# First loads of a two-layer decoder trunk: x and the gate-up columns moved to two other DMA queues

## The chip, the cores and the metric

The kernel runs on one core of a Trainium2 chip. The metric is the device time of one execution in microseconds (us), lower is better; the median of three runs is given. The engines are PE (TensorE), DVE (VectorE), ACT (ScalarE), POOL (GpSimd) and SP (SyncE), which here only issues DMAs.

## The reference

The program computes two decoder layers on one sequence of 512 tokens with 1024 features, in float32. Layer 0 mixes tokens by chunked gated linear attention, layer 1 by a sparse attention with three branches; each mixer is followed by a mixture of 16 experts with two chosen per token. Only the beginning of layer 0 matters here, cut from the reference:

```python
proj = x @ w_in                      # q, k, v, g_low (16 columns), r
q, k, v, g_low, r = jnp.split(proj, cuts, axis=-1)
log_a = jax.nn.log_sigmoid((g_low @ w_gate_up + b_gate).astype(f32)) / GLA_TAU
b = jnp.cumsum(chunks(log_a, DK), axis=3)
q_dec = q * jnp.exp(b)
scores = jnp.einsum('bhnid,bhnjd->bhnij', q_dec, k * jnp.exp(-b))
```

## The kernel before, in words

A float32 product is made of three float16 products: every operand is split into a high half (ACT writes it: L231 for x, L178 for a weight) and a low half (DVE subtracts: L232, L180), and PE adds high·high, high·low and low·high.

Weights come in units of 1 MB, 128 partitions by 2048 floats (`fetch`, L166), into three staging buffers `wst`. `split` makes the halves `whl` in four pieces of 512 columns. A staging buffer is free again when DVE has made the last low half of its unit. The unit of W[0], the first to be used, is itself fetched in four pieces (256 KB each), and ahead of each piece the callback `x_in` fetches a quarter of the transposed x (`xs`, 512 KB, L446).

The function `gla` begins so, in the order of the text: the small constants `small_gla` are fetched (L134); ACT makes the low-rank weights `wl` from them (L437), DVE their low half (L438); POOL clears `wgu` (L440); then come the eight loads of x and W[0]; four loads of the gate-up columns `wgu` (L454, 32 KB each); the unit W[2]; and the splits. PE then takes the quarters of x one after the other: per quarter six low-rank products into `low` (L465) and twelve into the two banks of q (L470). ACT copies `low` to `glow` (L475), PE multiplies it by `wgu` (L498), DVE and ACT make the gates from that (L506 to L522), while PE projects k of heads 0 and 1 from W[2] (L247 to L249), and then q and k of heads 2 and 3 from W[1] and W[3], whose splits DVE runs among the gates.

The order of the text is not the order on an engine. A planner of the framework lays the instructions of each engine out before the run, by their place in the text and by when it thinks that their operands are there; an instruction whose operands are late lets later ones pass. The order so made is fixed in the program.

Each DMA that SP or ACT issues signals one of eight completion counters in turn, and the next one on the same counter waits at its issue for the earlier one to land.

Of the kernel before, what the change touches and what calls it, by code (L numbers as in the profile page):

```python
# [22 lines left out]
S = 512  # L23
# [36 lines left out]
class Trunk:  # L60
# [368 lines left out]
    def gla(self):  # L429
        nc, a = self.nc, self.a  # L430
# [8 lines left out]
        wgu = self.tmp([P, 512], F32, "wgu", 1)  # L439
        nc.gpsimd.memset(wgu, 0.0)  # L440
        xT = [self.ph.tile([P, KT, S], F16, name=f"xT{i}", tag="xT", bufs=2) for i in range(2)]
        xs = []

        def x_in(c):
            xs.append(self.xtile("xs"))
            nc.sync.dma_start(xs[c], a["xT"][:, 2 * c * S:(2 * c + 2) * S])  # L446

        def x_split(c):
            k = slice(2 * c, 2 * c + 2)
            self.hilo(xT[0][:, k, :], xT[1][:, k, :], xs[c].rearrange("p (k t) -> p k t", k=2))  # L450

        unit = self.fetch(W[0], cuts=WCH, each=x_in)
        for i in range(4):
            nc.sync.dma_start(wgu[32 * i:32 * i + 16, :], a["gla_gu"])  # L454
        unit2 = self.fetch(W[2])
        wq = [self.split(unit, each=x_split), None]

# [1224 lines left out]
```

## Time and profile before

| | us |
|---|---|
| median of three runs | 954.7 |
| lowest and highest of them | 953.49, 954.93 |
| the profiled execution's own time | 952.24 |
| its span, first to last instruction | 950.5 |
| PE busy in the span | 877.9 (92%) |
| DVE, ACT, POOL busy | 744.7, 555.7, 310.8 |

A profile is one execution; its span begins with the first instruction and times below count from there. "Idle before" is the time in which an engine sat still ahead of an instruction, and the arrow names what ended it. Issues of DMAs are listed under the issuing engine's queue (SPq, ACTq) and are not counted as busy.

### The profile page before, as it was taken

To read this page: it belongs to the slowest core of one execution; us is meant where nothing else is said; L and a number is where in the kernel's file an instruction comes from. 1 tells how busy PE (TensorE), PEld (TensorE's weight loads), DVE (VectorE), ACT (ScalarE), POOL (GpSimd) and SP (SyncE) were. 2 spreads that over 40 slices of the span, in tenths; PEclk is the share of its full clock that TensorE was granted. 3 is DMA by queue.
4 is the path that set the end of the run, shared out by engine and by line. 5 is a ranking of instruction groups with operands and counts; after the bars stand their busy time and mean duration, and the time that the engine had idled before them with its cause. 6 is when DMAs were issued, how large, how long until landed. Compare 5 with 4: busy or idle time off the path is not lost. (4 is left out here: it accounts for less than half of the span.)

```text
span 950.5 us, 26582 instructions
## 1 busy us (share of the span) xinstructions
PE 877.9 (92%) x11218; PEld 718.4 (76%) x11218; DVE 744.7 (78%) x1666; ACT 555.7 (58%) x1174; POOL 310.8 (33%) x349
## 2 busy tenths in 40 slices
PE   6999999996799999899989998999999669999994
PEld 2468888876698989668978885767888568888871
DVE  5972225889899999798678765689777899999967
ACT  4823324424499999724644437784544449999940
POOL 0210021003435241530254524543430348623153
PEclk9999999998899999999999999979999879999997
DMA  8662322072399998871322001120005549999683
GB/s 294 247 205 84 128 90 89 1 300 86 114 374 408 377 378 314 212 205 46 134 89 90 1 3 45 52 85 1 2 2 225 219 180 384 404 369 378 238 156 111
DMA packets 29278, 169.19 MB, mean 178 GB/s; under 512 B 3521, under 2 KB 4161, under 8 KB 12641
## 3 DMA queue, kind: packets, MB, share of 16 engines
q1 hardware_dynamic: 23168, 144.49, 40.0%
q0 software_dynamic: 3072, 12.72, 6.0%
q10 hardware_dynamic: 2912, 10.23, 2.8%
q8 instruction: 90, 1.47, 0.6%
q14 instruction: 36, 0.29, 0.1%
HBM read 153.91 MB, written 13.50 MB: 176 GB/s over the span
## 5 line engine op out<-in xcount | busy, mean ns | idle before, releaser
L834 POOL TENSOR_SCALAR ohe<-icap,rt_px 128x96 f16<-128x96 f32 x112 | 114.1, 1033 | 132.8 <-PE bank L923 124.4
L180 DVE SCALAR_TENSOR_TENSOR whl<-wsu,whl 128x512 f16<-128x512 f32 x192 | 127.2, 714 | 2.9 <-ACT whl L178 2.8
L180 DVE SCALAR_TENSOR_TENSOR whl<-wst,whl 128x512 f16<-128x512 f32 x116 | 75.5, 702 | 67.4 <-ACT whl L178 67.4
L178 ACT ACTIVATE whl<-wsu 128x512 f16<-128x512 f32 x192 | 106.7, 624 | 3.2 <-PE bank L258 3.2
L845 PE MATMUL bank<-ohe,xs 128*128 128x96 f16 x2048 | 99.1, 212 | 6.6 <-DVE ohe L834 5.5
L178 ACT ACTIVATE whl<-wst 128x512 f16<-128x512 f32 x144 | 80.8, 624 | 33.1 <-PE bank L249 9.8
L845 PEld LDWEIGHTS <-xs 128*128 128x128 f16 x2048 | 94.5, 101 | 7.2 <-DVE ohe L834 4.5
L180 DVE SCALAR_TENSOR_TENSOR wha<-wst,wha 128x512 f16<-128x512 f32 x144 | 94.1, 705 | 3.1 <-ACT wha L178 3.0
L258 PE MATMUL bank<-whl,xt 128*128 128x256 f16 x320 | 87.1, 273 | 1.0 <-DVE xt L232 1.0
L256 PE MATMUL bank<-whl,xt 128*128 128x256 f16 x320 | 87.2, 273 | 0.8 <-ACT xt L231 0.7
L257 PE MATMUL bank<-whl,xt 128*128 128x256 f16 x320 | 87.2, 273 | 0.0
L178 ACT ACTIVATE wha<-wst 128x512 f16<-128x512 f32 x144 | 79.8, 623 | 3.4 <-DMA wst<-moe 3.2
L920 PE MATMUL bank<-xh,whl 128*128 128x96 f16 x576 | 75.2, 207 | 0.0
L918 PE MATMUL bank<-xh,whl 128*128 128x96 f16 x576 | 75.2, 207 | 0.0
L919 PE MATMUL bank<-xh,whl 128*128 128x96 f16 x576 | 75.2, 207 | 0.0
L258 PE MATMUL bank<-whl,oT 128*128 128x256 f16 x256 | 69.7, 273 | 1.6 <-DVE oT L232 1.6
L256 PE MATMUL bank<-whl,oT 128*128 128x256 f16 x256 | 69.8, 273 | 0.5 <-ACT oT L231 0.5
L258 PE MATMUL bank<-whl,xT 128*128 128x256 f16 x256 | 69.8, 273 | 0.0
L257 PE MATMUL bank<-whl,xT 128*128 128x256 f16 x256 | 69.8, 273 | 0.0
L256 PE MATMUL bank<-whl,xT 128*128 128x256 f16 x256 | 69.8, 273 | 0.0
L257 PE MATMUL bank<-whl,oT 128*128 128x256 f16 x256 | 69.8, 273 | 0.0
L919 PE MATMUL bank<-xh,wha 128*128 128x96 f16 x448 | 61.3, 210 | 0.8 <-PEq L986 0.8
(405 smaller groups left out, 2751.9 us busy)
## 6 DMA issues: line engine op xcount, KB each, us to landing
wsu<-moe SPq DMA_DIRECT2D x54, 1024.0 KB, 8.2
wst<-moe SPq DMA_DIRECT2D x42, 1024.0 KB, 7.8
wst<-gla_in SPq DMA_DIRECT2D x11, 1024.0 KB, 4.8
yslots<-y ACTq DMA_DIRECT2D x26, 384.0 KB, 7.0
wst<-nsa_in SPq DMA_DIRECT2D x9, 1024.0 KB, 4.9
wst<-gla_out SPq DMA_DIRECT2D x4, 1024.0 KB, 4.7
wha<-nsa_out SPq DMA_DIRECT2D x4, 1024.0 KB, 4.8
xs<-xT SPq DMA_DIRECT2D x4, 512.0 KB, 6.8
```

What stands on the lines that cost most here:

```text
L178: self.hi_ins = nc.scalar.activation(hl[:, 0, s], st[:, s], AF.Copy, scale=WS)
L180: nc.vector.scalar_tensor_tensor(hl[:, 1, s], st[:, s], WS, hl[:, 0, s], op0=OP.mult, op1=OP.subtract)
L256: nc.tensor.matmul(out, xt[0][:, k], w[0][:, s], start=(k == 0), stop=False)
L257: nc.tensor.matmul(out, xt[0][:, k], w[1][:, s], start=False, stop=False)
L258: nc.tensor.matmul(out, xt[1][:, k], w[0][:, s], start=False, stop=(k == KT - 1))
L834: eng.tensor_scalar(part[e][0][:, t], self.icap, self.px[:, t, e:e + 1], None, op0=OP.is_equal)
L845: nc.tensor.matmul(banks[half][:, j * CAP:(j + 1) * CAP], xs[t][:, i, k * P:(k + 1) * P], oh[:, t], start=(j == 0 and t == self.order[0] a ...
L918: nc.tensor.matmul(o, w[0][:, s], xh[:, 0, k], start=(k == 0), stop=False)
L919: nc.tensor.matmul(o, w[1][:, s], xh[:, 0, k], start=False, stop=False)
L920: nc.tensor.matmul(o, w[0][:, s], xh[:, 1, k], start=False, stop=(k == KT - 1))
```

## The change

The four loads of x are issued by ACT in place of SP, and the four loads of the gate-up columns by POOL in place of SP. The weights stay on SP. Nothing else is edited.

```diff
         def x_in(c):
             xs.append(self.xtile("xs"))
-            nc.sync.dma_start(xs[c], a["xT"][:, 2 * c * S:(2 * c + 2) * S])
+            nc.scalar.dma_start(xs[c], a["xT"][:, 2 * c * S:(2 * c + 2) * S])
...
         unit = self.fetch(W[0], cuts=WCH, each=x_in)
         for i in range(4):
-            nc.sync.dma_start(wgu[32 * i:32 * i + 16, :], a["gla_gu"])
+            nc.gpsimd.dma_start(wgu[32 * i:32 * i + 16, :], a["gla_gu"])
         unit2 = self.fetch(W[2])
```

## Rows read from the trace of the kernel before

**Rows 1.** Waits of PE over the whole span: total us, times, longest.

```profile
PE bank L759 <- DVE rt_o L746: 18.8, 4, 6.3
PE bank L465 <- ACT xT L231: 7.4, 1, 7.4
...
PE bank L249 <- DVE whl L180: 1.2, 1, 1.2
```

**Rows 2.** Timeline of PE, 0 to 24 us: start, length, instruction, count.

```profile
7.38 0.58 PE L465 MATMUL bank<-xT,wl 128*32 128x512 f16 x1 [7.38 <-ACT xT L231]
7.90 0.61 PE L470 MATMUL bank<-xT,whl 128*128 128x512 f16 x1
...
9.58 3.74 PE L470 MATMUL bank<-xT,whl 128*128 128x512 f16 x11
13.25 0.61 PE L465 MATMUL bank<-xT,wl 128*32 128x512 f16 x6
...
20.26 2.76 PE L470 MATMUL bank<-xT,whl 128*128 128x512 f16 x12
22.86 1.45 PE L498 MATMUL bank<-glow,wgu 128*128 128x512 f32 x3
```

**Rows 3.** Timeline of ACT, 0 to 24 us.

```profile
2.68 1.28 ACT L437 ACT_TABLE_LOAD   x1 [2.68 <-DMA small_gla<-small_gla]
3.98 0.31 ACT L437 ACTIVATE wl<-small_gla 128x128 f16<-128x128 f32 x1
6.27 1.06 ACT L231 ACTIVATE xT<-xs 128x1024 f16<-128x1024 f32 x1 [1.98 <-DMA xs<-xT]
7.23 0.61 ACT L178 ACTIVATE whl<-wst 128x512 f16<-128x512 f32 x1
8.31 1.06 ACT L231 ACTIVATE xT<-xs 128x1024 f16<-128x1024 f32 x1 [0.46 <-DMA xs<-xT]
...
17.81 2.19 ACT L178 ACTIVATE whl<-wst 128x512 f16<-128x512 f32 x4 [2.54 <-DMA wst<-gla_in]
```

**Rows 4.** Timeline of the SP queue, 0 to 30 us: the issues of DMAs.

```profile
0.81 0.38 SPq L134 DMA_DIRECT2D small_gla<-small_gla  x1
1.25 0.42 SPq L446 DMA_DIRECT2D xs<-xT  x1
1.72 0.42 SPq L166 DMA_DIRECT2D wst<-gla_in  x1
...
6.32 2.95 SPq L454 DMA_DIRECT2D wgu<-gla_gu  x4
10.71 0.35 SPq L166 DMA_DIRECT2D wst<-gla_in  x1
...
15.01 6.31 SPq L166 DMA_DIRECT2D wst<-gla_in  x3
```

**Rows 5.** DMA issues by line, one stretch each: 1.2 to 1.6, 1.6 to 2.1 us; last, to landing.

```profile
xs<-xT SPq DMA_DIRECT2D x1, 512.0 KB, 5.0
...
wst<-gla_in SPq DMA_DIRECT2D x1, 256.0 KB, 5.2
```

**Rows 6.** The line that issues yslots, whole span: ACT's DMA issues, ns min/median/max.

```profile
L959 ACTq DMA_DIRECT2D yslots<-y x26: 310/310/349, 263.8 to 900.3; - x26
```

**Rows 7.** Timeline of POOL, 0 to 90 us.

```profile
0.95 0.53 POOL L440 MEMSET wgu<- 128x512 f32 x1
...
2.46 0.23 POOL L483 IOTA io<- 128x128 int32 x1
40.49 0.41 POOL L539 COPY q<-qd 128x256 f32<-128x256 f32 x1 [37.80 <-DVE dec L522]
```

**Rows 8.** DMA issues by line, whole span, a row issued by POOL; last, to landing.

```profile
wst<-ck POOLq DMA_DIRECT2D x2, 1024.0 KB, 10.9
```

**Rows 9.** Timeline of DVE, 0 to 24 us.

```profile
1.41 0.48 DVE L480 MEMSET seg<- 128x512 f32 x1
...
4.32 0.29 DVE L438 SCALAR_TENSOR_TENSOR wl<-small_gla,wl 128x128 f16<-128x128 f32 x1 [2.28 <-ACT wl L437]
```

**Rows 10.** Timeline of DVE, 20 to 60 us.

```profile
21.41 0.17 DVE L672 TENSOR_SCALAR br<-br 128x16 f32<-128x16 f32 x1
23.92 0.75 DVE L506 TENSOR_SCALAR gate<-bank,small_gla 128x512 f32<-128x512 f32 x1 [2.35 <-PE bank L498]
...
28.49 0.68 DVE L180 SCALAR_TENSOR_TENSOR whl<-wst,whl 128x512 f16<-128x512 f32 x1
...
29.69 1.89 DVE L180 SCALAR_TENSOR_TENSOR whl<-wst,whl 128x512 f16<-128x512 f32 x3
...
45.41 0.68 DVE L180 SCALAR_TENSOR_TENSOR whl<-wst,whl 128x512 f16<-128x512 f32 x1
```

**Rows 11.** Timeline of ACT, 20 to 60 us.

```profile
22.95 0.63 ACT L178 ACTIVATE whl<-wst 128x512 f16<-128x512 f32 x1 [1.79 <-DMA wst<-gla_in]
```

## The prediction

> **What bounds the kernel now.** I read the waits of PE first, since PE is busy 92% of the span. The list is short: the longest single wait is the very first, 7.4 us until the first high half of x is there [rows 1]. The timeline of PE then shows what this start is worth [rows 2]: from 7.38 us on PE works through the four quarters of x almost without a hole, at 13.25 us it takes up the second quarter, at 20.26 us the last twelve products of q, at 22.86 us the gate product L498. So the later quarters don't matter by themselves: they are ready before PE wants them (the second high half of x starts at 8.31 us [rows 3], PE comes to it at 13.25). What sets PE's start is the first quarter alone.
>
> The timeline of ACT takes that back one step: ACT has been idle since L437 and starts the first high half at 6.27 us, released by the landing of xs [rows 3]. High half 1.06 us, and PE starts at 7.38 [rows 2, 3]. The first piece of W[0] isn't waited for: L178 follows L231 on ACT with no idle. The queue of SP shows when xs was asked for: behind small_gla, at 1.25 us; the weight piece at 1.72 [rows 4]; they land 5.0 and 5.2 us later, at 6.25 and 6.92 [rows 5].
>
> A second place where loading might count is PE's only other wait of this stretch, 1.2 us in front of an L249 for a low half [rows 1]; DVE delivers it with the L180 at 45.41 us [rows 10]. DVE is late there because it runs the gates from 23.92 us on, and those wait for PE's L498 [rows 10]. So this hole moves with PE's start, unless DVE's order changes. Where PE is shifted at the start, I carry the shift to the end: no row of PE's waits names a DMA, and DVE and ACT, which it does wait for, are fed by PE.
>
> **The change part by part.** The sum is made on the profiled execution, 952.24 us with a span of 950.5; the median of the runs is 954.7, 2.46 us above it, and I move the median by the sum.
>
> *x leaves SP's queue.* SP issues one DMA per 0.47 us (1.25 to 1.72 [rows 4]). On ACT nothing is ahead of the four x loads if the planner lets them pass L437, which waits until 2.68 us [rows 3]. The first one then goes out when SP issues small_gla, at 0.81 in place of 1.25: **-0.44 us**. The first weight piece takes the place of xs on SP: 0.47 us earlier.
>
> *What the issues cost ACT.* Four at 0.31 us (the issue of yslots, [rows 6]) to 0.42 (the same load on SP, [rows 4]) end at 2.05 to 2.5 us, before small_gla releases the table load at 2.68. Were they twice as slow, L437 would end near 6 us, still ahead of xs at 6.25. The cover is ACT's idle 1.98 us before L231 [rows 3]. I take **0**.
>
> *Two queues at once.* Before, xs is ahead of the weight piece in one queue, and the piece lands 0.65 us after it. Now both are under way together. No row of before shows x and weights side by side on two queues, so I bound it. Below: nothing is taken from xs, 0. Above: the whole first weight piece passes ahead of or between xs, **+0.65 us** for xs. If xs instead keeps its place and the piece is held until the second quarter of x is in (8.31 us, less the 0.44), then L178 starts at 7.87 in place of 7.23, +0.64 on PE's L470: the same size. small_gla (66 KB) stands in front of the piece on SP's queue, and the piece is issued 0.44 us after xs, so only part of it can cut in; I take a little over a third, **+0.24**.
>
> Here the Trainium skill speaks against the change: "DMA: Bandwidth & Descriptors", section Issuing engines are not separate DMA queues, says that DMAs started by different engines run on the same 16 DMA engines and interleave, so that only the sequencer's time to issue is saved. By that rule alone the sum would be at most the first term. No run here shows it yet.
>
> *Does an earlier start move PE one to one?* Eleven products of the first quarter take 3.74 us where twelve of the last take 2.76 [rows 2]; PE begins slow. If the quicker pace begins at the same moment as before, a start that is 0.44 earlier is worth half, 0.22. This lies within the bounds above.
>
> *The gate-up columns on POOL.* POOL clears wgu by 1.48 us, is done with its small work at 2.69 and then idle for 37.8 us [rows 7]. The columns are wanted at 22.86 us. A POOL-issued load of 1 MB lands 10.9 us after its issue [rows 8]; four of 32 KB, even one after the other at a quarter of that, land by 14. **0**; the cover is 8 us.
>
> *SP's queue behind them.* wgu's first issue waited until 6.32, when xs landed, and the unit W[2] until 10.71 [rows 4], since every SP load from the tenth on waits for the one eight places earlier. Without the four wgu loads W[2] takes the place of the first: about 6.3 us, 4.4 earlier. W[1] (15.01) follows its own chain and comes some 4 us earlier, so its split need not wait for the DMA at 22.95 [rows 11]. The price: 1 MB more is under way beside the later quarters of x. At most it costs them the time of 1 MB; the last quarter has PE's slow progress as cover. PE gains nothing, since W[2]'s high halves were done at 20.0 us [rows 3], wanted only behind L498, and the DVE work that makes the hole at 46 us stands behind L498. **0**.
>
> Sum: -0.44 + 0.24 = -0.2 us, bounds -0.44 and +0.21. That gives 954.5, between 954.3 and 954.9. About 0.2% (1.9 us) is what a measurement of this kernel can tell from no change; the three runs themselves lie 1.44 us apart.
>
> **The rivals.**
>
> *A, the forecast: the first quarter moves by a few tenths and nothing else does.* 954.5. For it: the whole change is in the first 15 us, of which PE sees only the first quarter. Chance 0.57.
>
> *B, W[1] fills DVE's hole.* DVE is idle for 2.35 us before 23.92 [rows 10]. W[1]'s low halves take 0.68 + 1.89 us and now stand among the gates, at 28.49 and 29.69 [rows 10]. With W[1] there 4 us earlier the planner can put them into the hole; DVE is then over 2 us ahead, and the 1.2 us of PE's wait go. 954.5 - 1.2 = 953.3, and with the full issue gain 953.0. Against it: it needs the planner, which decides by its own idea of arrivals, to change the order. Chance 0.15.
>
> *C, slower: x goes behind L437 on ACT.* In the text L437 comes before the x loads, and it waits for small_gla, loads a table and ends at 4.29 us [rows 3]. If ACT issues x only then, xs is asked for at 4.29 in place of 1.25, +3.04 us, and all of PE follows: 957.7. It decides at one point, the first ACT instruction of the program. Against it: on DVE a later memset (L480, 1.41 us) ran ahead of L438, which waits for the same constants [rows 9], so a waiting instruction lets ready ones pass. Chance 0.10.
>
> *D, the planner lays out something else differently downstream.* Unit splits go in groups of four on DVE, 0.68 + 1.89 = 2.6 us [rows 10]; one such group before or after the routing chain for which PE waits 18.8 us in four places [rows 1] is worth 2.6 us either way: 951.9 or 957.1. Earlier weights fill holes more often than they make them. Chance 0.18: 0.12 faster, 0.06 slower.
>
> *That it does nothing at all* (the queues share so that xs lands as before) gives 954.7 and is part of A.
>
> **How the numbers follow.** Likeliest is A, 954.5. Its own range is 954.2 to 955.0. The range for 8 in 10 takes in A, B and most of D with the spread of the runs: 952.3 to 957.0; it leaves out C and D's ends. Faster by over 0.2% (below 952.8): D's faster part, and about half of B through the spread of the runs, 0.12 + 0.07 = 0.19. Slower by over 0.2% (above 956.6): C and D's slower part, 0.16. Within: 0.65.
>
> **What would show it.** Right: four xs issues on ACT's queue from about 0.8 us, before L437; L231 of the first quarter within 5.8 to 6.5 us; PE's first L465 1.1 us later; W[2] issued near 6.3 us on SP; wgu landed long before L498; L498 starting at 22.4 to 23.1 us; the L249 wait of about 1.2 us still there. B: L180 of W[1] before the first L506, and no L249 wait. C: x issued after 4.2 us. D: the same span up to 50 us, and a different list of PE's waits behind it. The prediction is wrong where L498 moves by more than 0.7 us, or where PE's waits after 50 us change in sum by over 1.5 us.

## The result, and the profile after

The kernel became slower: median 961.94 us of six runs (958.25 to 963.29), against 953.94 for the kernel before in the same comparison (six runs, 950.82 to 954.93). The medians differ by 8.0 us; the ratio on record is 1.0092, 95% interval 1.0072 to 1.0112, which is 6.9 to 10.7 us. The median is above the range of 952.3 to 957.0. The profiled execution took 963.29 us, its span is 961.6.

I read the waits of PE first again (total us, times, longest). The first two stand almost as in [rows 1]; the third is new, and the L249 wait of [rows 1] is gone:

```profile
PE bank L759 <- DVE rt_o L746: 18.8, 4, 6.3
PE bank L465 <- ACT xT L231: 7.5, 1, 7.5
PE bank L550 <- DVE kd L532: 5.7, 1, 5.7
```

The timeline of PE after, to be read against [rows 2]:

```profile
8.48 0.61 PE L470 MATMUL bank<-xT,whl 128*128 128x512 f16 x1 [0.44 <-ACT whl L178]
...
9.99 4.15 PE L470 MATMUL bank<-xT,whl 128*128 128x512 f16 x11
14.07 0.61 PE L465 MATMUL bank<-xT,wl 128*32 128x512 f16 x6
...
23.69 3.60 PE L498 MATMUL bank<-glow,wgu 128*128 128x512 f32 x8
...
48.50 2.08 PE L550 MATMUL bank<-qd,kd 128*128 128x128 f32 x8 [5.67 <-DVE kd L532]
50.50 1.97 PE L553 MATMUL bank<-qd,gate 128*64 128x128 f32 x8
52.40 1.12 PE L561 MATMUL bank<-identf,gate 128*128 128x128 f32 x4
```

The same three groups in the timeline of PE before:

```profile
41.83 1.05 PE L550 MATMUL bank<-qd,kd 128*128 128x128 f32 x8
42.82 1.09 PE L553 MATMUL bank<-qd,gate 128*64 128x128 f32 x8
43.84 0.66 PE L561 MATMUL bank<-identf,gate 128*128 128x128 f32 x4
```

The shift of PE grows in three steps: 0.83 us at L498 (23.69 against 22.86 [rows 2]), 6.7 at L550, 8.6 at L561. Not only does PE wait for 5.7 us; the three groups behind the wait also take about twice as long. The table by stage shows why (window: its length, busy us of PE, PEld, DVE, ACT and POOL, then the granted clock, DMA share, GB/s):

```profile
48.00:50.00 2.00, 1.50 (x7) 1.51 (x8) 2.00 (x6) 2.00 (x5) 1.09 (x3) 0.50 0.00 0
50.00:52.00 2.00, 2.00 (x10) 1.77 (x10) 2.00 (x6) 0.53 (x2) 1.00 (x2) 0.50 0.00 0
52.00:54.00 2.00, 2.00 (x9) 1.22 (x8) 2.00 (x5) 0.00 (x0) 1.95 (x1) 0.50 0.00 0
54.00:56.00 2.00, 2.00 (x10) 0.89 (x9) 2.00 (x5) 0.85 (x2) 0.98 (x2) 0.94 0.02 4
```

After its idle time PE ran at the lower level, 1.2 GHz (0.50), for about six microseconds. The sum: +0.83 up to L498; +5.67 wait; the slow groups +1.01 (L550 to L553: 2.00 us apart, 0.99 before), +0.88 (L553 to L561: 1.90 against 1.02) and about 0.7 behind; -1.2 for the L249 wait that is gone. That is 7.9. The first L256, the next stage, starts at 74.31 against 66.26, +8.05, and at the first L759 (239.14 against 231.07) it is still +8.07. This agrees with the 8.0 us of the medians. The profiled execution is another 3 us longer behind that point; the medians don't show those, and they stay unexplained.

Why were `kd`, and so L550, late? DVE's timeline after, to be read against [rows 10]:

```profile
22.91 1.87 DVE L180 SCALAR_TENSOR_TENSOR whl<-wst,whl 128x512 f16<-128x512 f32 x3
27.11 2.50 DVE L180 SCALAR_TENSOR_TENSOR whl<-wst,whl 128x512 f16<-128x512 f32 x4 [2.32 <-ACT whl L178]
29.52 0.74 DVE L506 TENSOR_SCALAR gate<-bank,small_gla 128x512 f32<-128x512 f32 x1
31.45 0.69 DVE L180 SCALAR_TENSOR_TENSOR whl<-wst,whl 128x512 f16<-128x512 f32 x1 [1.19 <-ACT whl L178]
```

Before, the first L506 came at 23.92, straight behind L498, with all of W[1] and W[3] after it. Now eight low halves, W[1]'s (up to 24.8) and W[3]'s (27.11), stand ahead of it, and a ninth, of W[4], ahead of the first L507. PE's order of instructions is the same in both traces; DVE's and ACT's are not. The gates start 5.6 us later, since DVE sits at the L180 group until ACT has its high halves. They then stop once more, 1.19 us in front of W[4]'s low half, so that the first L507 starts at 32.06 against 24.70, 7.4 us later. ACT's timeline, against [rows 3, 11]:

```profile
0.81 0.89 ACTq L446 DMA_DIRECT2D xs<-xT  x2
4.68 1.28 ACT L437 ACT_TABLE_LOAD   x1 [4.68 <-DMA small_gla<-small_gla]
5.46 0.84 ACTq L446 DMA_DIRECT2D xs<-xT  x2
5.97 0.31 ACT L437 ACTIVATE wl<-small_gla 128x128 f16<-128x128 f32 x1
6.35 1.06 ACT L231 ACTIVATE xT<-xs 128x1024 f16<-128x1024 f32 x1
7.80 0.63 ACT L178 ACTIVATE whl<-wst 128x512 f16<-128x512 f32 x1 [0.39 <-DMA wst<-gla_in]
...
14.40 1.06 ACT L231 ACTIVATE xT<-xs 128x1024 f16<-128x1024 f32 x1 [4.15 <-DMA xs<-xT]
...
16.42 1.06 ACT L231 ACTIVATE xT<-xs 128x1024 f16<-128x1024 f32 x1 [0.45 <-DMA xs<-xT]
...
26.44 2.19 ACT L178 ACTIVATE whl<-wst 128x512 f16<-128x512 f32 x4 [3.61 <-DMA wst<-gla_in]
```

The 26.44 is the landing of W[3]. (W[4] landed only at 30.8.) SP's queue, against [rows 4], shows when it was asked for: the last group, 19.36, where before it was 16.46:

```profile
16.46 0.33 SPq L166 DMA_DIRECT2D wst<-gla_in  x1
```

After:

```profile
1.25 2.77 SPq L166 DMA_DIRECT2D wst<-gla_in  x5
...
10.90 0.33 SPq L166 DMA_DIRECT2D wst<-gla_in  x1
12.31 4.56 SPq L264 DMA_DIRECT2D x<-x  x3
19.36 10.60 SPq L166 DMA_DIRECT2D wst<-gla_in  x4
```

W[3] uses the staging buffer of W[0], which is free when DVE has made W[0]'s last low half: at 19.34 us now, 16.43 before. In DVE's timeline it is the L180 of the first line before, and the first of five in the second line, after:

```profile
15.75 0.68 DVE L180 SCALAR_TENSOR_TENSOR whl<-wst,whl 128x512 f16<-128x512 f32 x1
18.65 3.09 DVE L180 SCALAR_TENSOR_TENSOR whl<-wst,whl 128x512 f16<-128x512 f32 x5
```

That half stands behind the last quarter of x (16.42 on ACT; 13.52 before), and two of the four quarters were issued only behind L437. Before, W[3] landed at 25.4 us, hardly earlier, but there its split stood behind the gates' first step and held up none of it. So the start of a theory: the planner, seeing x off SP's queue, put two splits and a piece of a third ahead of the gates, and of these W[3]'s and W[4]'s were late.

### The profile page after: what moved, and what is told of

Its sections match the earlier page's. It is cut to its first block, busy times and chain, and to the rows that moved or that the text cites. A ratio compares the mean times of both kernels' runs of the same rounds, so it can differ in the third digit from the quotient of the medians.

```text
span 961.6 us, 26592 instructions
## 1 busy us (share of the span) xinstructions
PE 883.8 (92%) x11218; PEld 722.1 (75%) x11218; DVE 743.4 (77%) x1666; ACT 556.1 (58%) x1174; POOL 311.9 (32%) x353
## 5 line engine op out<-in xcount | busy, mean ns | idle before, releaser
L180 DVE SCALAR_TENSOR_TENSOR whl<-wst,whl 128x512 f16<-128x512 f32 x116 | 75.5, 701 | 73.2 <-ACT whl L178 73.2
L180 DVE SCALAR_TENSOR_TENSOR whl<-wsu,whl 128x512 f16<-128x512 f32 x192 | 127.0, 711 | 2.4 <-ACT whl L178 2.2
L178 ACT ACTIVATE whl<-wsu 128x512 f16<-128x512 f32 x192 | 106.7, 624 | 3.2 <-PE bank L258 3.2
L178 ACT ACTIVATE whl<-wst 128x512 f16<-128x512 f32 x144 | 80.5, 624 | 37.8 <-PE bank L249 11.7
L180 DVE SCALAR_TENSOR_TENSOR wha<-wst,wha 128x512 f16<-128x512 f32 x144 | 93.8, 700 | 2.9 <-ACT wha L178 2.9
L256 PE MATMUL bank<-whl,xt 128*128 128x256 f16 x320 | 87.2, 273 | 0.5 <-ACT xt L231 0.4
L178 ACT ACTIVATE wha<-wst 128x512 f16<-128x512 f32 x144 | 79.8, 623 | 3.6 <-DMA wst<-moe 3.4
L256 PE MATMUL bank<-whl,oT 128*128 128x256 f16 x256 | 69.7, 273 | 0.5 <-ACT oT L231 0.5
L256 PE MATMUL bank<-whl,xT 128*128 128x256 f16 x256 | 69.8, 273 | 0.0
```

The lines of the kernel that those rows point to most:

```text
L178: self.hi_ins = nc.scalar.activation(hl[:, 0, s], st[:, s], AF.Copy, scale=WS)
L180: nc.vector.scalar_tensor_tensor(hl[:, 1, s], st[:, s], WS, hl[:, 0, s], op0=OP.mult, op1=OP.subtract)
L256: nc.tensor.matmul(out, xt[0][:, k], w[0][:, s], start=(k == 0), stop=False)
```

## The experiments

In each comparison the kernel before ran on the same chip.

**Each part alone.** Only x on ACT:

```diff
-            nc.sync.dma_start(xs[c], a["xT"][:, 2 * c * S:(2 * c + 2) * S])
+            nc.scalar.dma_start(xs[c], a["xT"][:, 2 * c * S:(2 * c + 2) * S])
```

> Only the loads of x move to ACT's queue; the gate-up columns stay on SP. Theory P (order): the planner puts the splits of W[1] and W[3] in front of the gates on DVE and ACT, W[3] lands late, the gates wait, PE waits at L550 for kd and then runs at half clock: +6 to +9 us against before, the L550 wait 4 to 6.5 us. Rival Q (queues): two queues share the DMA engines and PE merely starts later: +0.8 to +1.5 us, no L550 wait above 1 us. Rival R (columns): the loss comes from POOL's loads, so this kernel is within 1 us of before.

Measured 957.77 against 953.59, ratio 1.0040 (1.0012 to 1.0068). The eight L180 ahead of the first L506 are there, so moving x is what changes the order. The theory's sizes (+6 to +9 us, a wait of 4 us or more) did not come: W[3] was issued at 16.72 and landed at 24.13, L506 started at 27.21, and PE's wait at L550 is only 1.8 us, with the granted clock at 1.00 behind it. In its place the start is late, 9.39 against 7.38 us. ACT's timeline shows the fourth issue of x holding up the first high half:

```profile
7.90 0.33 ACTq L446 DMA_DIRECT2D xs<-xT  x1
8.28 1.06 ACT L231 ACTIVATE xT<-xs 128x1024 f16<-128x1024 f32 x1 [2.12 <-DMA xs<-xT]
```

The x that L231 needs had landed by 5.2 us (4.4 us after its issue at 0.81). The fourth issue went out when the second load of x landed: asked for at about 1.3 us, it took 6.6 us, so it was in at 7.9 (DMA view, last column):

```profile
xs<-xT ACTq DMA_DIRECT2D x1, 512.0 KB, 6.6
```

This fits a wait at the issue for the earlier load on the same completion counter; in the second profile of this kernel, below, the second load landed 6.4 us after its issue and the fourth went out at 7.64. This is close to rival C: not x behind L437, but L231 behind an issue of x that came late. In this profile the first L256 is 2.5 us late: 1.76 at L498, +1.8 for the new wait, -1.2 for the old.

Only the gate-up columns on POOL:

```diff
-            nc.sync.dma_start(wgu[32 * i:32 * i + 16, :], a["gla_gu"])
+            nc.gpsimd.dma_start(wgu[32 * i:32 * i + 16, :], a["gla_gu"])
```

> Only the gate-up columns move to POOL; x stays on SP. Theory P: no split of a unit stands before the gates' first step L506 on DVE, so L506 follows L498 as before: -1.5 to +0.5 us, the L249 wait of 1.2 us at most kept; W[2] is issued near 6.3 us in place of 10.7. Rival Q: 0 (PE's start untouched). Rival R: +4 us or more.

Measured 952.48 against 953.59, ratio 0.9989 (0.9968 to 1.0011): no difference that can be told. DVE's first gate instruction again follows L498 (which started at 21.80), with a single L180 behind it:

```profile
22.86 0.75 DVE L506 TENSOR_SCALAR gate<-bank,small_gla 128x512 f32<-128x512 f32 x1 [2.35 <-PE bank L498]
23.53 0.68 DVE L180 SCALAR_TENSOR_TENSOR whl<-wst,whl 128x512 f16<-128x512 f32 x1
```

Neither wait (L249, L550) is there, and in the profile the first L256 starts at 64.16, 2.1 us earlier than before. The runs don't show such a gain, though their interval allows it.

**The order undone.** The full change, with W[3]'s split held behind the gates' last L507 and L508:

```diff
-                nc.vector.scalar_tensor_tensor(az, zb, -1.0, zb, op0=OP.mult, op1=OP.min)
-                last = nc.scalar.activation(az, az, AF.Exp)
+                self.gmin = nc.vector.scalar_tensor_tensor(az, zb, -1.0, zb, op0=OP.mult, op1=OP.min)
+                last = self.gexp = nc.scalar.activation(az, az, AF.Exp)
...
-                wq = [self.load_unit(W[i]) for i in (1, 3)]
+                wq = [self.load_unit(W[1]), self.load_unit(W[3], (self.gexp, self.gmin))]
```

> The full change, with the split of W[3] held behind the gates' L507 on DVE and L508 on ACT. Theory P: L506 runs right behind L498 again, the L550 wait of 5.7 us and the half clock behind it are gone; only the later start stays: +0.3 to +1.5 us against before. Rival Q: the loads are as late as in the changed kernel, so +5 us or more stays. Rival R: the same as Q.

Measured 953.42 against 953.59, ratio 1.0007 (0.9988 to 1.0025). No loss is left that can be told, with x and the gate-up columns still on the other queues and W[3] still going out as late, at 19.20. DVE comes to the gates at

```profile
25.06 0.75 DVE L506 TENSOR_SCALAR gate<-bank,small_gla 128x512 f32<-128x512 f32 x1 [0.43 <-PE bank L498]
```

right behind L498 (24.00). W[4]'s low half no longer stands ahead of L507 either, so the run does not separate the two splits. No L550 wait is left, and the L249 wait is 0.2 us. The start is late by more than in the changed kernel (+1.14 at L498); the L249 wait pays for it, and the first L256 comes at 66.40 against 66.26.

**The order alone.** The queues as before, and only the splits of W[1] and W[3] put ahead of the gates by hand:

```diff
-                gates()
+                wq2 = [self.load_unit(W[i]) for i in (1, 3)]; self.g_after = [self.hi_ins, self.lo_ins]; gates()
...
-                nc.vector.tensor_scalar(zb, Z[h], sm["gbg"][:, h:h + 1], None, op0=OP.add)
+                with self.behind(self.g_after[1] if h == 0 else None): nc.vector.tensor_scalar(zb, Z[h], sm["gbg"][:, h:h + 1], None, op0=OP.add)
```

> All loads stay on SP as before; the splits of W[1] and W[3] are put in front of the gates by hand. Theory P: the order alone costs it: W[3] lands near 25.4 us, its low halves end near 28.7, L506 starts there in place of 23.9, PE waits 3 to 5 us at L550 and runs at half clock behind that: +3 to +7 us. Rivals Q and R: within 1 us of before, since no queue is touched.

Measured 958.22 against 953.59, ratio 1.0052 (1.0036 to 1.0068): about 5 us lost without a load moved to another queue. DVE's timeline repeats the pattern of the changed kernel:

```profile
27.06 2.49 DVE L180 SCALAR_TENSOR_TENSOR whl<-wst,whl 128x512 f16<-128x512 f32 x4 [1.21 <-ACT whl L178]
29.48 1.40 DVE L506 TENSOR_SCALAR gate<-bank,small_gla 128x512 f32<-128x512 f32 x2
```

PE waits 4.3 us at L550, the clock falls to 0.56 and 0.58 in the windows behind it, and the first L256 is 4.6 us late. W[3] landed at 26.4 us here, and no piece of W[4] stands ahead of a gate's step; the order with a late W[3] is enough for most of the loss.

**Why W[3] was late.** Two candidates: its staging buffer (late quarters of x), and the three row loads of x (1.5 MB) beside it on SP's queue. Full change, with L437 held behind all four x loads:

```diff
-            nc.scalar.dma_start(xs[c], a["xT"][:, 2 * c * S:(2 * c + 2) * S])
+            self.xs_in = nc.scalar.dma_start(xs[c], a["xT"][:, 2 * c * S:(2 * c + 2) * S])
...
-        nc.scalar.activation(wl[:, 0, :, 0:16], gl_in, AF.Copy, scale=WS)
...
         unit2 = self.fetch(W[2])
+        with self.behind(self.xs_in): nc.scalar.activation(wl[:, 0, :, 0:16], gl_in, AF.Copy, scale=WS)
```

> The full change, with the table load and the low-rank weights of ACT held behind all four loads of x (in the changed kernel two of the loads stand behind them, at 5.5 and 5.8 us); the splits of W[1] and W[3] stay in front of the gates. Theory S (slot): the late last quarters of x make the low halves of W[0] late, these free the staging buffer that W[3] needs, so W[3] is fetched at 19.36 us; with all of x asked for by 3 us W[3] goes out near 17, the gates begin 2 us earlier and about half of the 8 us stays: +2.5 to +5.5 us against before. Rival T (rows): W[3] waits behind the three loads of x's rows on SP: these stay ahead of it, so the loss stays at +7 to +9.

Measured 960.42 (four runs) against 952.24, ratio 1.0089 (1.0058 to 1.0121). The edit did what it should: the x loads go out by 4.86 us and W[3] at 16.42, three microseconds sooner. Yet W[3] landed at 28.21, 11.8 us after its issue, and the L550 wait is 6.4 us. SP's queue shows what ran beside it:

```profile
13.45 2.89 SPq L264 DMA_DIRECT2D x<-x  x3
16.42 15.30 SPq L166 DMA_DIRECT2D wst<-gla_in  x4
```

POOL's zero fill of yslots (three of 384 KB, from 16.82) is under way then too. The buffer alone is not the cause: the +2.5 to +5.5 us expected by it were missed. Full change, with the row loads of x and the two rows of the norm held behind W[3]:

```diff
-            self.nc.sync.dma_start(self.x[t], self.a["x"][t * P:(t + 1) * P, :])
+            with self.behind(self.w3_in): self.nc.sync.dma_start(self.x[t], self.a["x"][t * P:(t + 1) * P, :])
...
-                wq = [self.load_unit(W[i]) for i in (1, 3)]
+                wq = [self.load_unit(W[i]) for i in (1, 3)]; self.w3_in = self.dma_ins
```

> The full change, with the loads of x's rows held behind W[3]'s on SP. Theory S: W[3] still waits for the buffer of W[0], so it is issued at 19 to 19.5 us and the loss stays: +6.5 to +9 us against before. Rival T: W[3] is issued near 11 to 12 us, lands ahead of the gates, and the loss falls to +2 us or less.

Measured 958.28 against 952.24, ratio 1.0052 (1.0029 to 1.0074). W[3], issued at 19.20 because of its buffer, landed in 5.3 us, at 24.56 (7.1 us in the changed kernel). L506 starts at 27.64 and the L550 wait is 4.3 us. Between a quarter and two fifths of the loss is back, by the medians (6.0 of 8.0 us left), the first L256 (5.6 of 8.1) or the ratios (5.0 of 8.8); both ranges expected are missed. Two things blur this run. W[4]'s low half, ahead of L507, still waits 1.70 us for its weight. And the planner moved more than the edit names: POOL's three zero fills of yslots, which the changed kernel issues from 20.04 us, now go out at 19.88, 48.66 and 52.89, so the row loads and two of the fills left W[3]'s side together. Which of them slowed it isn't shown. Each edit alone explains less than the whole, so I ran both together:

> The full change with both edits: all four loads of x ahead of ACT's table load, and the loads of x's rows behind those of the weights; DVE and ACT keep the order of the changed kernel up to the end of the gates, with the splits of W[1], W[3] and the first piece of W[4] in front of them. Theory S+T (the landing of W[3] alone decides, and it is its buffer and the loads beside it that set it): W[3] is issued near 16.5 us, lands by 22 to 23 us, L506 starts within 2 us of L498's first result, PE waits at most 2.5 us at L550, and the loss falls to +0 to +3 us. Theory P in its narrow form (the order costs whenever the splits stand in front of the gates, whenever the load lands): PE waits 4 us or more at L550, +5 us or more.

Measured 952.65 against 952.30, ratio 1.0007 (0.9989 to 1.0025). W[3] was issued at 16.27 and landed in 5.8 us. In the timeline, ACT's split of W[3], then DVE's first gate, which still stands behind all eight L180:

```profile
22.07 2.19 ACT L178 ACTIVATE whl<-wst 128x512 f16<-128x512 f32 x4 [0.33 <-DMA wst<-gla_in]
...
25.15 0.74 DVE L506 TENSOR_SCALAR gate<-bank,small_gla 128x512 f32<-128x512 f32 x1
```

The L550 wait is 1.5 us and the clock stays at 1.00. W[4]'s low half, still ahead of L507, starts at 25.87 without a wait. The first L256 comes at 66.05 against 66.26: PE reached L498 0.55 us sooner than before (22.31), and the L249 wait of 1.2 us is gone. So the planner's order with the weights there in time costs nothing that can be measured; the theory that the order as such costs is too wide. Here too two of the fills came late, at 44.45 and 48.68.

**What could be gained.** The gate-up columns on POOL, and W[1]'s split alone ahead of the gates, where rival B would have it:

```diff
+            nc.gpsimd.dma_start(wgu[32 * i:32 * i + 16, :], a["gla_gu"])
...
+                wq2 = [self.load_unit(W[1])]; self.g_after = [self.hi_ins, self.lo_ins]; gates()
...
+                wq = wq2 + [self.load_unit(W[3])]
```

> Only the gate-up columns move to POOL, and the split of W[1] alone is put in front of the gates by hand. Theory P: with W[2] issued early W[1] lands by 19 to 20 us, its low halves fill DVE's hole in front of L506, the gates start right behind L498 and the L249 wait is gone: -0.5 to -2.5 us against before. If W[1] lands later than 21 us the gates wait for it: 0 to +2.

Measured 952.06 against 952.24, ratio 1.0003 (0.9986 to 1.0020). The L249 wait is gone and the first L256 starts at 65.58, 0.7 us sooner than before; the runs don't show that much, and the gain of 0.5 to 2.5 us expected of it was missed. No version that I ran beats the kernel before by more than its measurement is uncertain.

**The spread of x alone.** The kernel with only x on ACT had run between 952.78 and 958.82; the question was whether its slower runs have the lower clock behind L550. The same kernel again, unedited:

> The kernel with only x on ACT once more, for a second profile: its runs fell into two groups, near 953 and near 958 us, and its profile was of the lower one. Theory C (clock): in the upper group PE's wait at L550 is longer than 1.8 us and the granted clock falls to 0.5 for some us behind it; in the lower group it stays at 1.0. Rival: the groups come from the later stages, with the same clock around 45 us in both.

Measured 957.40 against 952.24, ratio 1.0050 (1.0031 to 1.0069), which confirms the loss. The profiled run is now one of the slower, 956.53, and its profile again has a short wait at L550 (1.6 us), the clock at 1.00 and PE starting at 9.13 us; the first L256 is 2.0 us late. So the theory of the clock behind L550 fails, and its rival holds: the two profiles are 0.4 us apart at the first L256 (68.72 and 68.31) and 2.6 us the other way at the first L1272 (450.9 and 453.5). Between them, from 400 to 420 us, the granted clock was 1.00 in the first and 0.80 and 0.86 in the second. The kernel before spreads in the same way. In the first comparison of x_act its 12 runs with a granted clock of 0.968 or more, taken over the whole run, average 951.3 us and its 17 below that 954.8; x_act's four and four average 954.5 and 958.2. At like clocks the loss is 3.2 to 3.4 us, where the profiles show 2.5 and 2.0; the rest stays open.

## Why the prediction was wrong, and where it was right

**The step that failed** is "SP's queue behind them", taken as **0**, with its reading in rival B. It argued that W[1] and W[2] would come about 4 us earlier, as they did (W[2] issued by 4.0 us, W[1] at 10.90), and that "its split need not wait". It left two things out. First, the planner goes by its own idea of arrivals: it moved not only W[1]'s split into DVE's hole, where it fitted (done at 24.8), but W[3]'s and a piece of W[4]'s too, and W[3]'s staging buffer came free 2.9 us later than before, not sooner. On engines that work in a fixed order, a split whose weight is late holds up all behind it: here the gates, then `kd`, then PE. Second, rival D sized a moved group at 2.6 us, DVE's busy time. Counted from L498, the first L507 came 6.5 us later than before: about 3.0 us are moved work (2.4 of W[3], 0.6 of W[4]) and 3.5 are waits in it (2.3 and 1.2). PE felt 5.7 of it at L550, and then 2.6 us more from its clock. The loss in full needs the order and the late weight: with the order undone 1.0007, with the weights early 1.0007, with the order and no queue touched 1.0052.

**The start**, forecast at -0.2, came out at +0.83 at L498, outside its bounds of -0.44 and +0.21 and past the 0.7 us that the prediction named as a sign of being wrong. ACT's issues cost next to nothing here, but not for the reason given: the last two went out from 5.46 to 6.30 us, not by 2.5, just ahead of L231 at 6.35, and with x alone on ACT they cost 2 us. The first xs landed sooner: issued at 0.81 and there 4.6 us later, at 5.4 in place of 6.25 [rows 5]. The DMA view shows where the price went (last column: us to landing):

```profile
xs<-xT ACTq DMA_DIRECT2D x1, 512.0 KB, 4.6
small_gla<-small_gla SPq DMA_DIRECT2D x1, 66.0 KB, 3.8
```

small_gla landed at 4.6 in place of 2.6 us. It takes 1.8 or 1.9 us in the four profiles with x on SP, and 3.3 to 3.9 in the seven with x on ACT, where x goes out beside it. L437 waited for it, and ACT, busy with L437 until 6.28, took up the landed quarter at 6.35. I had counted "the cover is ACT's idle 1.98 us" without asking what the change does to the load on which that cover rests. The first weight piece was in at 7.79 instead of 6.92. This is the sharing that I had bounded: its second branch had L178 at 7.87 and +0.64 on PE's L470, and L178 came at 7.80, the first L470 0.58 later. But the sum of bounds was wrong: +0.21 is 0.65 less the 0.44 of the earlier issue, and the 7.87 had that 0.44 in it already, so the upper bound should have been +0.64. The other 0.25 us come from the run of eleven, which began 0.41 later and took 4.15 us in place of 3.74, so the second quarter began 0.82 late (14.07 against 13.25 [rows 2]). That part may be chance: over the runs these eleven took between 3.05 and 4.65 us, and 4.15, 4.36 and 4.65 in three kernels whose first loads are issued alike (the changed one, the one with the rows held, the one with W[3] held).

The rule of the Trainium skill that spoke against the change ("DMA: Bandwidth & Descriptors", Issuing engines are not separate DMA queues) agrees with the trace. From 0.8 to 8 us the core's DMA engines moved 236 GB/s before and 236 after: the second queue moved no more bytes in that time, it only let x pass small_gla and the weight piece.

**Rival C** did not come about as put: two of the x issues passed L437, two came behind its table load, the third at 5.46 us, just when the first x load had landed (5.4). The late two didn't hold up PE at the quarters themselves, as the prediction says of them; they cost at the far end, through W[0]'s buffer.

**Right** were the gate-up columns on POOL at 0 (landed by 11.5 us at the latest, and alone no loss) and W[2]'s earlier issue. B's signs, L180 of W[1] ahead of L506 and no L249 wait, did come, but with the opposite outcome: they don't tell a filled hole from a new wait. D's signs, the same span up to 50 us and other waits behind it, missed the place; the new wait ends at 48.5.

## What to carry to other kernels

Moving a load to another queue changes more than its own issue: where a planner lays out the order of in-order engines, compare that order before and after, and ask of each work that has moved forward whether its operand's buffer, not only its queue, is free sooner. Price a moved instruction by its own time and the wait that it can bring with it, plus the lower clock when PE idles for some microseconds. When a load is moved off a queue, list the small loads that it was behind: here a 66 KB constant took 3.8 us in place of 1.8 once x went beside it, and the first instruction of ACT hung on it.

## What the hardware showed that I had not expected

- The granted clock fell to 0.50 behind PE waits of 4.3 to 6.4 us, to 0.56 and 0.58 in the windows of one of those runs, and stayed at 1.00 behind waits of 1.5 to 1.8 us. The clock cost about 2.6 us where the wait was 5.7. No run here has a wait between 1.8 and 4.3 us at this place.
- The same 1 MB load, W[3], landed 5.3, 5.8, 7.1, 7.4, 8.9 (before), 10.7 (the order alone) and 11.8 us after its issue, with different loads under way beside it. Issued at nearly the same time, 19.20 and 19.36, it took 5.3 us without the row loads and two of the fills, and 7.1 with them.
- An issue of a DMA can hold up the computing behind it on its engine: on ACT the first high half came at 8.28 us, behind the fourth x load at 7.90, though the x that it needed had landed by 5.2 us. That fourth issue itself went out when the second x load had landed, at 7.9.
